# Two accumulator tiles for the attention, a turned gate column, and weight splits with a fixed place: three edits to one block kernel

## The chip, the cores and the metric

The kernel runs on one core of one Trainium2 chip. The core's engines are TensorE (PE in the profile; PEld is its weight load), VectorE (DVE), ScalarE (ACT), GpSimd (POOL) and SyncE (SP). DMAs are issued from the queues of SP, ACT and POOL. The metric is the device time of one execution in microseconds; a kernel's time is the median of several runs. Beside these runs stands one profiled execution, from which every trace number comes.

## The reference

The reference is one block of a diffusion backbone: 512 latent tokens and 256 context tokens, model width 2048, one layer, float32.

```python
shift, scale, gate = jnp.split(silu_c @ w_ada[l] + b_ada[l], 3, axis=-1)
h = _modulate(_rmsnorm(xs, norm_g[l]), shift[:, None], scale[:, None])
...
p = h @ w_l
q = _rope(_rmsnorm(_heads(p, OFF_Q, N_Q_HEADS), q_norm_g[l]), cos, sin) * q_scale
k = _rope(_rmsnorm(_heads(p, OFF_K, N_KV_HEADS), k_norm_g[l]), cos, sin)
...
attn = _attention(q, jnp.concatenate([k, kc], axis=1), jnp.concatenate([v, vc], axis=1))
...
y_a = (attn * jax.nn.silu(z_a)) @ w_pa
y_b = (_fourier_mix(u_b) * jax.nn.silu(z_b)) @ w_pb
y = (g_a * y_a + g_b * y_b) @ w_o
new_xs = xs + gate[:, None] * y
```

A modulated norm feeds one wide projection. Of it come queries (12 heads of 128), keys and values (4 heads), two SiLU gates, two sigmoid gates and the input of a Fourier mixing. The attention runs over 768 keys. Each branch is projected to 2048, the two are merged by their sigmoid gates, and after one more projection the result is multiplied by "gate", a vector of 2048 numbers, added to the input and normed.

## The kernel before

**Products.** Every large product is exact to float32 by three float32r matmuls (mm3, lines 339 to 341): each factor is split into a high and a low part, and high x high, high x low and low x high are added up in one accumulator. The split itself (split_from, lines 181 and 182) is a ScalarE copy that writes the high part and a VectorE subtraction that writes the low one. It is done on chip for weights (tiles "whi" and "wlo" from a raw piece "wr" or "R" of 128x1024) and for activations.

**Weight stream.** All weights come through one list, "todo", of pieces in the order of use. load_more issues the loads while raw buffers are free; get(key) returns a split piece and on the way splits some pieces ahead of it (split_piece, line 265 on). A split needs one of three pairs of hi/lo buffers.

**Stages.** The trace shows the norm and the first products up to about 160 us, the eight groups of the large projection up to 803 us, the attention up to about 1005 us, and then branch A, the merge and the output projection up to the end. The projection groups keep their sums in the pool "psp" (names x and y, four pairs of two banks, which are the whole of PSUM). When they end, that pool is closed and "psq" is opened on the same eight banks: one tile "banks" of 128 x 8 x 512, of which banks[0] is the first six and banks[1] the last two. `wide` are four areas of 768 columns in the first six: three take scores in turn (next_wide), the fourth takes the turned probabilities. Bank 6 (fill_acc) is the accumulator of the Fourier branch; bank 7 takes the values' products and the turned queries.

**The attention's loop** runs over 48 steps, 12 heads by 4 blocks of 128 queries. A step holds: the scores of block i with their maximum (VectorE, L1533) and exponential (ScalarE, L1535); the values of an earlier pair of blocks; the turning of block i-1 (turn: six TensorE transposes, L1551, into the fourth wide area, then a split into "pth" by ScalarE and "ptl" by VectorE); the division of block i-1; and one or two of the 64 steps of the Fourier branch's projection (filler, fill). That projection runs over four chunks of 512 columns, in the order 0, 2, 1, 3; a chunk takes two weight pieces (key "pab") and 16 steps of three matmuls. At steps 10, 22 and 34 the keys and values of the next key head are fetched (get_keys), and with them the next chunk's two pieces are split ahead. At 16 of the steps a product of weights with the conditioning row (use_gate, L1369) leaves one column of the vector "gate" in gparts.

**After the loop** the two halves of gparts and a bias are added into gcol (128 x 16: number 128k+p of the vector stands in partition p, column k), and gcol is stored to the DRAM tile gs (16 x 128) on POOL's queue, in the order of gs's columns (L1744 to L1746). load_rows reads gs later as rows, spread over all partitions (L1783).

**What sets the order.** A planner places each engine's instructions from its own model of their durations, before anything runs; the order in the program is its priority. Within a manual_schedule block the order is that of the program; issue_after(i) queues what the block traces behind instruction i on i's engine, without waiting for i's end. PE is in manual order before the projection groups; in the attention nothing is, apart from a few issue_after. Each engine works its instructions strictly in the order planned, and waits at each for its semaphores. A pool with reuse_waits="tile" makes a tile wait for the former tiles that lay where it lies, and not for a whole former pool.

Of the kernel before, what the change touches and what calls it, by code (L numbers as in the profile page):

```python
# [10 lines left out]
F32 = mybir.dt.float32  # L11
F32R = mybir.dt.float32r
ACT = mybir.ActivationFunctionType
ALU = mybir.AluOpType
# [4 lines left out]
P = 128  # L19
# [3 lines left out]
KK = D // P  # L23
# [4 lines left out]
NKEY = T + C  # L28
KT = NKEY // P
# [44 lines left out]
def context_piece(g, name, pc):  # L74

    n = 28 * (g - NQZ) + 4 * ONE_GROUP.index(name) + pc
    if n % 2 == 0 and 0 <= n < 8:
        return "cn", n // 2
    if n % 7 == 4 and 18 <= n < 46:
        return "cr", n // 7 - 2  # L80
# [43 lines left out]
def block_kernel(ctx, tc, xT, ctx_rows, ctx_toks, x, c_row, w_ss, w_gate, vecs, qkg, rope, dft_c, dft_s,  # L124
                 w_start, w_g, w_pab, w_o, final_g, out):
    nc = tc.nc
# [6 lines left out]
    const = sb("const")  # L133
# [9 lines left out]
    gs = dsc.tile([KK, P], F32, name="gs")  # L143
# [13 lines left out]
    def uid(s):  # L157
        cnt[0] += 1
        return f"{s}{cnt[0]}"
# [20 lines left out]
    def split_from(src, hi, lo):  # L180
        first = nc.scalar.activation(hi, src, ACT.Copy)  # L181
        return first, nc.vector.tensor_tensor(lo, src, hi.bitcast(F32), op=ALU.subtract)  # L182
# [61 lines left out]
    def hl_tiles():  # L244
        if more_hl and not more_hl[0]:
            hl_pools.extend(range(MORE_HL))
            more_hl.clear()
        elif more_hl:
            more_hl[0] -= 1
        hl_pools.append(hl_pools.pop(0))  # L250
        pool = hl_pools[-1]
        if isinstance(pool, tuple):
            return [slot_tile(p, (1024,), F32R) for p in pool]
        if isinstance(pool, int):
            return int_tiles(pool)
        return [pool.tile([P, 1024], F32R, tag=t, bufs=hl_pools.count(pool), name=uid("w" + t)) for t in ("hi", "lo")]


    last_split, split_of, in_line, context_sub, chained = [], [], [], [], []

    look = [1]

    def split_piece(e):
        if e.out is not None or e.kind == "raw":
            return
        raws = [r for _, r in e.raws]
        src = raws.pop(0) if e.stage is None else chain[e.pc]
        for r in raws:
            nc.vector.tensor_tensor(src, src, r, op=ALU.add)
        if e.off:  # L270
            with ExitStack() as line:
                if e.key == ("P7", KV, 3):
                    line.enter_context(tc.issue_after(context_sub[-1].ins))
                if e.key[1] in DIFF_IN_LINE:

                    line.enter_context(tc.issue_after(split_of[-2][1].ins))
                nc.vector.tensor_tensor(src, chain[e.pc], src, op=ALU.subtract)
        hi, lo = e.dst() if e.dst else hl_tiles()
        if isinstance(hi, Halves):
            for k in range(2):  # L280
                last_split.append(split_from(src[:, 512 * k : 512 * k + 512].rearrange("p (a c) -> p a c", a=2),
                                             hi.parts[k], lo.parts[k]))
        else:
            hi, lo = hi[:, : e.cols], lo[:, : e.cols]
            with ExitStack() as line:
                if in_line:
                    for i in last_split[-1]:
                        line.enter_context(tc.issue_after(i.ins))
                last_split.append(split_from(src, hi, lo))
        split_of.append(last_split[-1])  # L290
        if e.nxt is not None:
            chained[:] = [nc.gpsimd.dma_start(chain[e.pc], e.nxt, accum_op=ALU.add)]  # L292
        if e.stage == 3:
            left[e.pc] = 0
        r = lambda t: t if isinstance(t, Halves) else t.rearrange("p (n m) -> p n m", n=e.n)
        e.out = (r(hi), r(lo))

    def get(key):
        load_more()
        turn = [e for e in ahead if not e.aside]  # L300
        assert turn[0].key == key, (turn[0].key, key)
        for e in turn[: min(look[0], len(hl_pools))]:
            if e is turn[0] or e.key[0] != "V":
                split_piece(e)
        load_more()
        e = turn[0]
        ahead.remove(e)
        free.extend(p[0::2] for p, _ in e.raws if p in retired)
        return e.raws[0][1] if e.kind == "raw" else e.out
# [17 lines left out]
    def take(shape, dt=F32, pool=None):  # L327
        p = next((p for p in free if p[0] is pool), free[0])
        free.remove(p)
        t = slot_tile(p, shape, dt)  # L330
        home[id(t)] = p, t
        return t

    def give(*ts):
        free.extend(home.pop(id(t))[0] for t in ts)
# [19 lines left out]
    cvt, bada, ng = small[:, : 2 * KK], small[:, 2 * KK : 5 * KK], small[:, 5 * KK :]  # L355
# [1 line left out]
    nc.vector.tensor_scalar(bsc1, bada[:, KK : 2 * KK], 1.0, None, op0=ALU.add)  # L357
    shift = const.tile([P, KK, 2], F32, name="shift")
    gain = const.tile([P, KK, 2], F32, name="gain")
    gcol = const.tile([P, KK], F32, name="gcol")  # L360
    gparts = const.tile([P, 2 * KK], F32, name="gparts")

    pairs = []
# [58 lines left out]
    for g in range(LAST + 1):  # L422
        for name in ONE_GROUP:
            if (g, name) == (LAST, "Q4"):
                stream_keys(0)
            if g == KV:
                f = CTX_FORMS.index(next(f for n, f, _, _ in PRODUCTS if n == name))
                stream(("cf", name), cf_d[:, :, f].rearrange("i p j c -> p i j c"), 1024, 8, dst=ctx_tiles)
            stream_product(name, g, w_g[g], BY_DVE_GATES if g else ())
            for pc in range(4):  # L430
                p = context_piece(g, name, pc)
# [4 lines left out]
            for pc in range(4):  # L436
                if (g, name, pc) in GATE_AT:
                    q = GATE_AT[g, name, pc]
                    stream(("gate", q), w_gate[q], 1024, 1, "raw")
                    e = todo.pop()  # L440
# [4 lines left out]
    q = NGATE  # L445
# [300 lines left out]
    def split_next():  # L746
        e = next(e for e in ahead if e.out is None and e.kind != "raw")
        split_piece(e)
        e.raws = []
# [27 lines left out]
    with tc.manual_schedule(engines={E.PE}):  # L777
# [6 lines left out]
        with tc.manual_schedule(engines={E.Activation, E.DVE}):  # L784
# [25 lines left out]
            for kb in range(1, 4):  # L810
                k = kb + 1
# [32 lines left out]
            for kb in range(4, KK - 4, 2):  # L844
# [6 lines left out]
                k = kb + 2  # L851
# [100 lines left out]
    for g in range(4):  # L952
        gate_b(g)
        positions(g)
        if g < 2:
            tokens(g + 2)
        with behind((finals[-1], low[g if g < 2 else 3])):
            for e in ahead[:g]:
                split_piece(e)
            for z, y in products[2 * g - 4 : 2 * g - 2] if g > 1 else ():  # L960
                nc.vector.tensor_tensor(z, y, z, op=ALU.mult)
# [18 lines left out]
    banks = []  # L980
# [478 lines left out]

    pgs.close()  # L1460
    psq = ctx.enter_context(tc.tile_pool(name="psq", bufs=1, space=PSUM, reuse_waits="tile"))
    whole_psum = psq.tile([P, 8, 512], F32, name="banks")
    banks += [whole_psum[:, :6, :], whole_psum[:, 6:, :]]
    last_y[:] = [0, 0]
    wide = [flat(banks[0])[:, NKEY * i : NKEY * i + NKEY] for i in range(4)]
    fill_acc, b1 = banks[1][:, 0, :], lambda: banks[1][:, 1, :]
# [49 lines left out]
    probs, pts, AT, A1, A2 = {}, {}, {}, {}, {}  # L1516
# [30 lines left out]
    def turn(i):  # L1547
        p = probs.pop(i)
        tp = wide[3]
        for k in range(KT):  # L1550
            nc.tensor.transpose(tp[:, k * P : (k + 1) * P], p[:, k * P : (k + 1) * P], ident)  # L1551
        if i % 2 == 0:
            pts[i // 2] = [atp.tile([P, KT, 256], F32R, tag=n, bufs=2, name=uid(n)) for n in ("pth", "ptl")]
        c = slice((i % 2) * P, (i % 2) * P + P)
        split_from(tp[:, :NKEY].rearrange("p (k q) -> p k q", k=KT), *(w[:, :, c] for w in pts[i // 2]))
        give(p)

    def values(half):
# [127 lines left out]
    for i in range(NSTEP + 3):  # L1686
# [13 lines left out]
        if 1 <= i <= NSTEP:  # L1700
            turn(i - 1)
            divide(i - 1)
# [5 lines left out]
        n = next((n for n, at in enumerate(SUM_AT) if at <= i < at + 3), None)  # L1708
# [8 lines left out]
        if i == 3:  # L1717
            with tc.issue_after(maxima[0].ins), tc.issue_after(maxima[1].ins):
                e = take((1024,))
# [8 lines left out]
        if i in GATE_STEPS:  # L1728
            n = NGATE + GATE_STEPS.index(i)
# [11 lines left out]
            next(first)  # L1741
    ats_.close()
    left[3] = 0
    nc.vector.tensor_tensor(gcol, gparts[:, :KK], gparts[:, KK:], op=ALU.add)  # L1744
    nc.vector.tensor_tensor(gcol, gcol, bada[:, 2 * KK :], op=ALU.add)
    nc.gpsimd.dma_start(gs.rearrange("k p -> p k"), gcol)  # L1746


    gp = ctx.enter_context(tc.tile_pool(name="gp", bufs=1, side="right", reuse_waits="tile"))
# [320 lines left out]
```

## Time and profile before

| | |
|---|---|
| median of 3 runs | 1285.94 us (1285.69 to 1288.67) |
| profiled execution | 1286.97 us, span of its instructions 1285.2 us, granted clock 0.999 |
| TensorE | 1269.6 us busy, 6562 matmuls |
| VectorE, ScalarE, GpSimd | 991.0, 683.2 and 173.2 us busy |
| DMA | 319.07 MB, mean 248 GB/s |

How to read the lines: "L339 PE MATMUL banks<-whi,s" is line 339 of the kernel, an instruction of TensorE that writes the tile "banks" and reads "whi" and "s" (numbers in tile names are left out). In a timeline the columns are the start and the duration in us, the engine and the instruction; behind it, in brackets, the idle time of the engine just before and what ended it ("<-ACT ev L1160"). A matmul's record is longer than its share of the stream, since the next one begins before it ends.

### The profile page before, as it was taken

What the parts mean: (1) busy time and instruction counts of PE and PEld (TensorE: products, weight loads), DVE (VectorE), ACT (ScalarE), POOL (GpSimd) and SP (SyncE); (2) the same over time, 40 slices, a digit from 0 to 9 for tenths busy, and PEclk for the clock granted to TensorE, in tenths of its full rate; (3) what the DMA queues carried; (4) which work ended last, traced back from release to release, by engine and by line L of the source; (5) the groups of instructions that cost most, each with busy time, mean ns of one, the idle gap of its engine ahead of it and who ended that gap; (6) DMA issues with size and microseconds to landing.
All of it is one profiled execution on the core that took longest, in us unless ns stands there. A gap on an engine that the chain in (4) does not pass through costs nothing.

```text
span 1285.2 us, 17638 instructions
## 1 busy us (share of the span) xinstructions
PE 1269.6 (99%) x6562; PEld 1045.2 (81%) x6562; DVE 991.0 (77%) x1305; ACT 683.2 (53%) x1077; POOL 173.2 (13%) x226
## 2 busy tenths in 40 slices
PE   8999999999999999999999999999999999999997
PEld 5677888888888888888888888888888888888886
DVE  5767899889778787748687756778898777787677
ACT  5322765555466564543355445766667646465544
POOL 0000121111102011012021011011100221211310
PEclk9999999999999999999999999999999999999999
DMA  9998798888898998887879897578852989998986
GB/s 378 412 368 344 242 204 254 229 240 239 234 315 209 320 271 254 291 197 188 282 204 288 254 259 234 180 234 250 265 178 67 260 241 258 245 207 222 227 207 179
DMA packets 104343, 319.07 MB, mean 248 GB/s; under 512 B 9889, under 2 KB 32801, under 8 KB 100289
## 3 DMA queue, kind: packets, MB, share of 16 engines
q1 hardware_dynamic: 54336, 195.24, 41.8%
q0 software_dynamic: 27600, 100.29, 37.0%
q10 hardware_dynamic: 22320, 22.42, 5.1%
q8 instruction: 51, 0.84, 0.3%
q14 instruction: 36, 0.29, 0.1%
HBM read 283.30 MB, written 34.61 MB: 247 GB/s over the span
## 4 chain that ended last, share of the span: by engine, by line
PE 82%; DVE 3%; DMA 2%; ACT 2%; issue 1%; SPq 0%; ACTq 0%
PE banks L339 10%; PE banks L340 10%; PE banks L341 10%; PE x L341 9%; PE x L339 9%; PE x L340 9%; PE y L341 8%; PE y L340 8%; PE y L339 8%; PE banks L1551 2%; DMA wr<-in_w_pab 1%; DVE wlo L182 1%; DMA s<-yb_d 1%; PE banks L1665 1%; DVE s L182 0%
## 5 line engine op out<-in xcount | busy, mean ns | idle before, releaser
L181 ACT ACTIVATE whi<-R 128x1024 fp32r<-128x1024 f32 x138 | 145.1, 1058 | 143.7 <-PE banks L341 47.5
L182 DVE TENSOR_TENSOR wlo<-R,whi 128x1024 fp32r<-128x1024 f32 x138 | 167.7, 1221 | 61.2 <-ACT whi L181 60.9
L182 DVE TENSOR_TENSOR wlo<-wr,whi 128x1024 fp32r<-128x1024 f32 (+1 forms) x122 | 147.3, 1213 | 62.7 <-ACT whi L181 62.5
L181 ACT ACTIVATE whi<-wr 128x1024 fp32r<-128x1024 f32 (+1 forms) x122 | 127.4, 1050 | 123.4 <-PE y L341 33.0
L339 PE MATMUL banks<-whi,s 128*128 128x512 f32 (+1 forms) x400 | 157.8, 394 | 0.9 <-ACT ev L1160 0.7
L340 PE MATMUL banks<-wlo,s 128*128 128x512 f32 (+1 forms) x400 | 155.9, 390 | 0.0
L341 PE MATMUL banks<-whi,s 128*128 128x512 f32 (+1 forms) x400 | 155.8, 389 | 0.0
L339 PE MATMUL x<-whi,s 128*128 128x512 f32 x352 | 137.1, 390 | 0.0
L341 PE MATMUL x<-whi,s 128*128 128x512 f32 x352 | 137.0, 389 | 0.0
L340 PE MATMUL x<-wlo,s 128*128 128x512 f32 x352 | 136.9, 389 | 0.0
L292 POOL DMA_DIRECT2D R<-in_w_g x68 | 59.5, 874 | 484.7 <-DVE wlo L182 290.2
L340 PE MATMUL y<-wlo,s 128*128 128x512 f32 x316 | 123.0, 389 | 0.1
L339 PE MATMUL y<-whi,s 128*128 128x512 f32 x316 | 122.9, 389 | 0.0
L341 PE MATMUL y<-whi,s 128*128 128x512 f32 x316 | 122.8, 389 | 0.0
L181 ACT ACTIVATE s<-wr 128x512 fp32r<-128x512 f32 (+2 forms) x93 | 60.8, 677 | 66.0 <-DMA wr<-cf_d 24.4
L182 DVE TENSOR_TENSOR s<-wr,s 128x512 fp32r<-128x512 f32 (+2 forms) x93 | 66.7, 749 | 31.8 <-ACT s L181 30.9
L339 PEld LDWEIGHTS banks<-whi,s 128*128 128x128 f32 x400 | 75.2, 188 | 16.6 <-ACT ev L1160 1.1
L341 PEld LDWEIGHTS banks<-whi,s 128*128 128x128 f32 x400 | 75.2, 188 | 15.3
L340 PEld LDWEIGHTS banks<-wlo,s 128*128 128x128 f32 x400 | 75.2, 188 | 13.9 <-DVE wlo L182 0.2
L340 PEld LDWEIGHTS x<-wlo,s 128*128 128x128 f32 x352 | 66.1, 188 | 13.8
L341 PEld LDWEIGHTS x<-whi,s 128*128 128x128 f32 x352 | 66.1, 188 | 13.7
L339 PEld LDWEIGHTS x<-whi,s 128*128 128x128 f32 x352 | 66.1, 188 | 13.6
(333 smaller groups left out, 2794.0 us busy)
## 6 DMA issues: line engine op xcount, KB each, us to landing
wr<-in_w_g SPq DMA_DIRECT2D x124, 512.0 KB, 5.6
R<-in_w_g POOLq DMA_DIRECT2D x68, 512.0 KB, 7.4
wa<-in_w_ss SPq DMA_DIRECT2D x31, 1024.0 KB, 9.5
R<-in_w_g SPq DMA_DIRECT2D x32, 512.0 KB, 5.8
wr<-in_w_gate SPq DMA_DIRECT2D x32, 512.0 KB, 5.1
wr<-in_w_o SPq DMA_DIRECT2D x24, 512.0 KB, 7.1
R<-in_w_o POOLq DMA_DIRECT2D x24, 512.0 KB, 8.9
wr<-in_w_pab SPq DMA_DIRECT2D x20, 512.0 KB, 6.1
```

The source lines that it names most:

```text
L181: first = nc.scalar.activation(hi, src, ACT.Copy)
L182: return first, nc.vector.tensor_tensor(lo, src, hi.bitcast(F32), op=ALU.subtract)
L292: chained[:] = [nc.gpsimd.dma_start(chain[e.pc], e.nxt, accum_op=ALU.add)]
L339: nc.tensor.matmul(o, ah, bh, start=start, stop=False, skip_group_check=cont)
L340: nc.tensor.matmul(o, ah, bl, start=False, stop=False, skip_group_check=cont)
L341: nc.tensor.matmul(o, al, bh, start=False, stop=stop, skip_group_check=cont)
L1551: nc.tensor.transpose(tp[:, k * P : (k + 1) * P], p[:, k * P : (k + 1) * P], ident)
L1665: last_turn[0] = nc.tensor.transpose(tp[:, k // 2, 256 * (k % 2) + P * t : 256 * (k % 2) + P * t + P], m[:, t, k * P : k * P + P], ident)
```

## The change

Three edits stand together.

1. The tile "banks" of eight banks becomes two tiles, of six and of two banks, at the same place. All views into them stay.
2. gcol becomes 128 x 32. The additions go in place into gparts, VectorE transposes gparts into gcol (blocks of 32 x 32: within each block of 32 partitions, column k becomes row k), and four DMAs on POOL's queue store rows of 32 numbers, 16 rows each, in place of the one.
3. Each turn's pair of split instructions is kept in the list turned_low. When a piece with the key "pab" is split, its two instructions are queued behind the pair that is the third last in the list at that time, ScalarE's behind ScalarE's and VectorE's behind VectorE's. For the first chunk's pieces the list is empty and nothing is queued.

```diff
-    last_split, split_of, in_line, context_sub, chained = [], [], [], [], []
+    last_split, split_of, in_line, context_sub, chained, turned_low = [], [], [], [], [], []
...
             with ExitStack() as line:
-                if in_line:
-                    for i in last_split[-1]:
-                        line.enter_context(tc.issue_after(i.ins))
+                for i in last_split[-1] if in_line else turned_low[-6:-4] if e.key[0] == "pab" else ():
+                    line.enter_context(tc.issue_after(i.ins))
                 last_split.append(split_from(src, hi, lo))
...
-    gcol = const.tile([P, KK], F32, name="gcol")
+    gcol = const.tile([P, 2 * KK], F32, name="gcol")
...
-    whole_psum = psq.tile([P, 8, 512], F32, name="banks")
-    banks += [whole_psum[:, :6, :], whole_psum[:, 6:, :]]
+    banks += [psq.tile([P, n, 512], F32, name=f"banks{n}") for n in (6, 2)]
...
-        split_from(tp[:, :NKEY].rearrange("p (k q) -> p k q", k=KT), *(w[:, :, c] for w in pts[i // 2]))
+        turned_low.extend(split_from(tp[:, :NKEY].rearrange("p (k q) -> p k q", k=KT), *(w[:, :, c] for w in pts[i // 2])))
...
-    nc.vector.tensor_tensor(gcol, gparts[:, :KK], gparts[:, KK:], op=ALU.add)
-    nc.vector.tensor_tensor(gcol, gcol, bada[:, 2 * KK :], op=ALU.add)
-    nc.gpsimd.dma_start(gs.rearrange("k p -> p k"), gcol)
+    nc.vector.tensor_tensor(gparts[:, :KK], gparts[:, :KK], gparts[:, KK:], op=ALU.add)
+    nc.vector.tensor_tensor(gparts[:, :KK], gparts[:, :KK], bada[:, 2 * KK :], op=ALU.add)
+    nc.vector.transpose(gcol, gparts)
+    for i in range(0, P, 32):
+        nc.gpsimd.dma_start(gs[:, i : i + 32], gcol[i : i + KK, :])
```

## The prediction, written before the result was known

> **What bounds the kernel now.** I read the page first: the busy line, the clock, the chain.
>
> ```profile
> PE 1269.6 (99%) x6562; PEld 1045.2 (81%) x6562; DVE 991.0 (77%) x1305; ACT 683.2 (53%) x1077; POOL 173.2 (13%) x226
> ...
> PEclk9999999999999999999999999999999999999999
> ...
> PE 82%; DVE 3%; DMA 2%; ACT 2%; issue 1%; SPq 0%; ACTq 0%
> ```
>
> TensorE works from end to end at full clock, and the chain lies on it for 82%. None of the three edits takes a matmul away, so all that can be won is time in which TensorE waits. The next view is the busy time by stretches (columns: length; then PE, PEld, DVE, ACT, POOL busy with counts; clock; DMA share; GB/s).
>
> ```profile
> 320.00:480.00 160.00, 160.00 (x710) 132.53 (x709) 128.01 (x179) 89.33 (x146) 20.45 (x22) 1.00 0.91 268
> 800.00:1010.00 210.00, 207.42 (x1363) 181.18 (x1363) 174.84 (x280) 143.01 (x272) 28.65 (x47) 1.00 0.65 195
> 1000.00:1100.00 100.00, 100.00 (x488) 84.17 (x487) 75.60 (x73) 56.06 (x61) 22.13 (x29) 1.00 0.97 257
> ```
>
> The projections (320 to 480 us) and the stage behind the attention (1000 to 1100 us) have no idle TensorE time; the attention (800 to 1010 us) has 210 - 207.42 = 2.58 us. The first row gives a yardstick too: 710 matmuls in 160 us are one each 0.225 us, while one record lasts 0.39 us (rows below). So a record covers the first 0.39 - 0.225 = 0.16 us of any gap, and a wait costs its idle time and 0.16 us. The third view lists TensorE's own waits from 800 us on, then from 1010 us on:
>
> ```profile
> PE banks L1389 <- DVE ptl L182: 0.8, 1, 0.8
> PE banks L339 <- ACT ev L1160: 0.7, 1, 0.7
> PE banks L1551 <- DVE ptl L182: 0.4, 1, 0.4
> PE banks L339 <- ACT s L1535: 0.4, 1, 0.4
> PE banks L339 <- DVE R L1499: 0.2, 1, 0.2
> ...
> PE banks L1665 <- DMA s<-yb_d: 0.7, 1, 0.7
> ```
>
> Five waits in the attention sum to 2.5 us, with 5 x 0.16 some 3.3 us; the one behind it is 0.9 us. That is all there is to see for a change of this kind: 4.2 us, 0.33% of the time.
>
> **Part 1, the banks as two tiles.** The timeline where the last projection group gives way to the attention:
>
> ```profile
> 795.39 0.69 DVE L182 TENSOR_TENSOR s<-y,s 128x512 fp32r<-128x512 f32 x1 [2.03 <-ACT s L181]
> ...
> 802.54 0.39 PE L341 MATMUL x<-whi,s 128*128 128x512 f32 x1
> ...
> 802.97 0.59 ACT L1160 COPY ev<-x 128x512 f32<-128x512 f32 x1 [1.66 <-PE x L341]
> ...
> 803.60 0.50 PE L339 MATMUL banks<-whi,s 128*128 128x512 f32 x1 [0.68 <-ACT ev L1160]
> ...
> 805.10 0.28 PE L339 MATMUL banks<-s,s 128*128 128x256 f32 x1
> ```
>
> The first matmul into "banks" comes 1.06 us after the last into "x", where 0.225 would do: 0.83 us lost. It is a matmul of the Fourier branch, and goes to bank 6 alone; but the one tile of eight banks stands on all the old accumulators and waits for the last reader of any, here ScalarE's copy out of an x. As two tiles, the two-bank one waits only for whoever held banks 6 and 7. The old pool made its two x pairs first, then the y pairs, so I take it for a y, whose last reader ended at 795.39 + 0.69 = 796.1. Then the six Fourier matmuls (803.60 to 805.10) start at 802.77 and cover the copy, which ends at 803.56; the scores, in the six-bank tile, find it done. If that cover were gone (the scores planned ahead of them), the wait would merely move to the scores. Bounds: -0.83 (cover holds) and 0 (an x lies there after all, or the order turns). I take -0.83: nothing in the row makes the six need more than bank and weights. No instruction is added.
>
> **Part 2, the gate columns.** It removes one DMA of 128 x 16 single numbers, adds one VectorE transpose of a 128x32 tile and three more DMAs on POOL's queue. The rows of today, in order: the second of the two additions, the store, the next POOL load; then the store's time to landing; then the first reader.
>
> ```profile
> 988.37 0.18 DVE L1745 TENSOR_TENSOR gcol<-gcol,small 128x16 f32<-128x16 f32 x1
> ...
> 989.01 1.20 POOL L1746 DMA_DIRECT2D gs<-gcol  x1 [14.92 <-DVE gcol L1745]
> 991.95 0.90 POOL L292 DMA_DIRECT2D R<-in_w_pab  x1 [1.74 <-DVE wlo L182]
> ...
> gs<-gcol POOLq DMA_DIRECT2D x1, 8.0 KB, 11.2
> ...
> 1091.87 0.55 POOL L1783 DMA_DIRECT2D s<-gs  x1 [5.30 <-DVE s L182]
> ```
>
> The store lands at 1000 us and is first read at 1091.87: 91 us cover whatever its time becomes, and 8 KB in 11.2 us can shrink only behind that cover. VectorE's transpose is not in the trace; the nearest rows bound it: 0.18 us (128x16) below, 0.42 us (the 128x256 subtractions) above. I take 0.2 us by its size; it falls where TensorE shows no wait, so 0 on the path, 0.42 if it meets one. POOL's four issues at 0.55 to 0.90 us are 2.2 to 3.6 us against 1.20: from 989.2 they end by 992.8, and the weight load at 991.95 goes out at most 0.9 us late. Its product is in the stage that has no idle time and a DMA share of 0.97 from 1000 us on, so -0.9 to +0.9 is the bound. I take 0.
>
> **Part 3, the splits behind their steps.** A Fourier weight piece is split in two by ScalarE (whi) and VectorE (wlo). Eight are split in all, in the order in which the branch uses them; these rows are of the whole, then of the fifth:
>
> ```profile
> L181 ACT ACTIVATE whi<-wr x8: 1049/1061/1077, 797.5 to 940.3; 128x1024 fp32r<-128x1024 f32 x8
> ...
> 836.09 6.13 DMA wr<-in_w_pab
> ...
> 842.30 1.07 ACT L181 ACTIVATE whi<-wr 128x1024 fp32r<-128x1024 f32 x1 [1.66 <-DMA wr<-in_w_pab]
> 843.27 0.88 ACT L1535 ACTIVATE s<-banks,gain 128x768 f32<-128x768 f32 x1
> ...
> 844.14 0.80 ACT L181 ACTIVATE pth<-banks 128x768 fp32r<-128x768 f32 x1
> ...
> 842.30 0.87 PE L1551 MATMUL banks<-ident,s 128*128 128x128 f32 x6 [0.40 <-DVE ptl L182]
> ...
> 845.99 0.44 PE L1389 MATMUL banks<-ident,wr 128*128 128x128 f32 x2 [0.82 <-DVE ptl L182]
> ```
>
> ScalarE stands 1.66 us for a load still under way; queued behind it are the next exponential and the next turned split (pth, 844.14), then VectorE's ptl, then TensorE at 845.99: 0.82 + 0.16 = 0.98 us. TensorE's other wait here, 0.40 + 0.16, ends at 842.30, before ScalarE goes on, so that load is not its cause. And nobody needs that piece yet: it is the first of the third chunk, the 33rd of the branch's 64 steps, and by 887.3 only 30 were done.
>
> ```profile
> L339 PE MATMUL banks<-whi,s x16: 389/395/501, 803.6 to 840.2; 128*128 128x512 f32 x16
> 847.27 0.40 PE L339 MATMUL banks<-whi,s 128*128 128x512 f32 x1
> ...
> L339 PE MATMUL banks<-whi,s x30: 387/396/501, 803.6 to 887.3; 128*128 128x512 f32 x30
> ...
> L181 ACT ACTIVATE pth<-banks x7: 807/812/815, 811.4 to 836.3; 128x768 fp32r<-128x768 f32 x7
> ...
> L181 ACT ACTIVATE pth<-banks x19: 802/812/815, 811.4 to 883.6; 128x768 fp32r<-128x768 f32 x19
> ...
> L181 ACT ACTIVATE pth<-banks x31: 802/812/816, 811.4 to 932.2; 128x768 fp32r<-128x768 f32 x31
> ```
>
> The pieces are split in the program at steps 10, 22 and 34, where 9, 21 and 33 score blocks have been turned; the pair [-6:-4] of the list is the third last of these: turns 6, 18, 30 (counted from 0), at 836.3, 883.6, 932.2. So the second chunk's two pieces may go from 837 (ScalarE) and 839 (VectorE), and at 1.2 us each on VectorE are done by 841.4; their first use is the 17th step, at 847.27: 5.9 us cover. The third chunk goes behind 883.6, the fourth behind 932.2. No queue is passed and no DMA added; raw buffers are held longer (the second chunk's first until 840), so what waits on SP for a free one starts later; late next would be a gate product or the next group's keys, and the planner's order on SP decides which. No row prices that; I let part 2's 0.9 us stand for it in the range. The sum by place:
> - 830 to 848: two splits now (pieces 4, 5), two after (3, 4), both landed long ago. The DMA wait goes: -0.98, and -1.54 if piece 4, now at 834, had made the other one. Two splits back to back put 1.2 us more between a pth and its ptl: +0.2 (1.2 - 0.98) at worst. I take -0.8, near the row of the removed wait.
> - 880 to 900: likewise two and two, without this wait:
>
> ```profile
> 895.38 1.06 ACT L181 ACTIVATE whi<-wr 128x1024 fp32r<-128x1024 f32 x1 [1.23 <-DMA wr<-in_w_pab]
> 897.87 0.50 PE L339 MATMUL banks<-whi,s 128*128 128x512 f32 x1 [0.22 <-DVE R L1499]
> 930.00:950.00 20.00, 19.64 (x132) 17.04 (x131) 18.32 (x30) 14.31 (x28) 2.01 (x4) 1.00 0.55 178
> ```
>
> TensorE's 0.22 + 0.16 goes: -0.4; bounds -0.4 and 0.
> - 930 to 950: one split now (the last), two after. VectorE is busy 18.32 of 20 us, and another 1.2 us leaves 0.5. Bounds 0 and +1.4 (1.2 + 0.16). A step's share of VectorE has 0.7 us free (174.84 busy of 210, over 48 steps of 4.4); I take +0.5, what is left of 1.2.
>
> Both waits, at 842.30 and 845.99, end with ptl, which frees the one area that score blocks are turned in. The Trainium skill ("Perfetto Trace Analysis", Optimization Strategy) reads the same gap recurring on the engine that should be saturated as a sign that there is not enough SBUF or PSUM for the next tile; by it the gap would come back at another step, and the sum would be 0.8 us less of a gain. The trace agrees for the 0.40 us at 842.30, which no load wait precedes, and not for the 0.82 us at 845.99, which one does.
>
> **Sum:** -0.83 + 0 - 0.8 - 0.4 + 0.5 = -1.5 us. The profiled execution took 1286.97 (span 1285.2 and 1.8 around it), 1.0 above the median of the runs, 1285.94. It would become 1285.5, and the median **1284.4**. A measurement of this kernel can tell about 0.3% from no change, 3.9 us here, so this is "no change". One cost stays out of the sum: the planner orders the attention anew from its own durations, which may move any small wait.
>
> **Rivals.**
> 1. **All waits go** (0.25). With no split in the way the planner's order holds: all five attention waits, 3.3, the branch wait, 0.9, and part of the gaps under 0.16 us that records cover (48 steps, at most 7.7; a sixth is 1.3): -5.5, 1280.4. For it: each wait is on a DVE or ACT that runs late. Against: the 0.4 us on L1535 and the one on yb_d have nothing to do with the edits.
> 2. **The wait comes back** (0.15). The one turning area is what limits: TensorE's wait for ptl returns a step later whatever ScalarE did, so only -0.83 and +0.5 are left: 1285.6. For it: both waits end with ptl. Against: the longer one has the load wait ahead of it. This is how the time would go by the Trainium skill's rule quoted above. That the whole change does nothing falls here too.
> 3. **Slower: the splits bunch** (0.10). With 0.7 us of VectorE free in a step, a split of 1.2 us needs two steps, and two need four. Where the planner puts both within fewer, next to the keys' split and a gate product (1.2 us), each split between pth and ptl holds TensorE 1.2 us. Four of the six so placed cost +4.9, less 0.83: 1290.0. It decides from two splits in under four steps, at 837, 885 or 933 us. For it: VectorE at 18.32 of 20. Against: today a gate product and a split stand back to back at 834, and TensorE's next wait comes 6 us later (842.30).
>
> ```profile
> 833.64 1.22 DVE L1369 SCALAR_TENSOR_TENSOR wr<-wr,crow 128x1024 f32<-128x1024 f32 x1
> ...
> 834.86 1.21 DVE L182 TENSOR_TENSOR wlo<-wr,whi 128x1024 fp32r<-128x1024 f32 x1
> ```
>
> **How the numbers follow.** The forecast has 0.50, its own range 1282.3 (-0.83 - 1.54 - 0.4 - 0.9 = -3.7) to 1288.8 (0 + 0.2 + 0 + 1.4 + 0.9 + 0.4 = +2.9), each with all bounds at one end. Low end of the range: rival 1 and part 2's 0.9, 1279.5. High end: just above the forecast's own, 1289.0, which leaves out rival 3 at its full price. Faster by over 0.3%: rival 1 and a tail of the forecast below 1282.1, 0.28. Slower: rival 3, 0.09. Within: the rest, 0.63.
>
> **What would show it.** Part 1: a first "banks" matmul 0.2 us behind the last x one, no wait on L1160. Part 2: gs landing in under 6 us and nothing else moved. Part 3: whi from wr in pairs behind turns 6, 18 and 30, none waiting for in_w_pab; TensorE idle in the attention under 1.5 us instead of 2.58. It is wrong if new waits on ptl stand at 837 to 848 or 932 to 948, or if the stage behind 1010 us moves by more than 1 us.

## The result, and the profile after: 15% slower

The changed kernel takes 1477.46 us (median of 5 runs, 1473.18 to 1477.97); the kernel before, run beside it, 1286.18 us. The ratio is 1.1476, 95% interval 1.1459 to 1.1494: 191 us slower, where 1284.4 us was forecast. The page of the changed kernel (busy line; then TensorE's busy tenths and its clock in 40 slices of 36.9 us):

```profile
span 1474.0 us, 17650 instructions
...
PE 1335.2 (91%) x6562; PEld 1079.9 (73%) x6562; DVE 1000.2 (68%) x1306; ACT 690.6 (47%) x1077; POOL 173.8 (12%) x229
...
PE   8999999999999999999999767777777988898996
...
PEclk9999999999999999999999888989988999999998
```

The 6562 matmuls are the same. The first 22 slices (to 811 us) are as before; then TensorE is idle about a quarter of the time in the attention, and its clock falls. Of the span's growth, 1474.0 - 1285.2 = 188.8 us, TensorE's idle time is (1474.0 - 1335.2) - (1285.2 - 1269.6) = 123.2 us, and its longer busy time 1335.2 - 1269.6 = 65.6 us. Two stages hold nearly all of it. The attention's 48 turned splits mark them, here of the kernel before, then of the changed one (minimum, median and maximum in ns; first and last start):

```profile
L181 ACT ACTIVATE pth<-banks x48: 796/812/828, 811.4 to 1003.7; 128x768 fp32r<-128x768 f32 x48
```

```profile
L181 ACT ACTIVATE pth<-banks x48: 792/810/815, 813.6 to 1143.7; 128x768 fp32r<-128x768 f32 x48
```

From the first to the last: 192.3 us before, 330.1 after, or 4.09 and 7.02 us a step (47 intervals): +137.8. From the last to the end of the span: 281.5 and 330.3: +48.8. With the 2.2 us up to the first that is 188.8. TensorE's largest waits in the changed kernel, four in the attention and one behind it (us in total, times, longest):

```profile
PE banks L338 <- DVE ptl L182: 49.0, 44, 2.9
PE banks L1549 <- ACT s L1533: 20.0, 15, 2.1
PE banks L338 <- ACT pth L181: 10.3, 12, 1.2
PE banks L1388 <- DVE ptl L182: 5.4, 3, 1.8
...
PE banks L338 <- DVE s L1108: 15.2, 6, 4.8
```

In the attention before, these were five waits of 2.5 us in all. Lines are one or two lower than before (338 for 339, 1549 for 1551, 1533 for 1535). One round of the attention shows what they are, in the timeline:

```profile
815.46 0.51 PE L338 MATMUL banks<-s,s 128*128 128x512 f32 x1 [0.81 <-DVE ptl L182]
...
816.81 0.96 DVE L1531 TENSOR_REDUCE gain<-banks 128x1 f32<-128x768 f32 x1 [1.41 <-PE banks L340]
...
817.80 0.90 ACT L1533 ACTIVATE s<-banks,gain 128x768 f32<-128x768 f32 x1 [3.40 <-DVE gain L1531]
...
818.85 1.54 PE L1549 MATMUL banks<-ident,s 128*128 128x128 f32 x6 [2.08 <-ACT s L1533]
...
820.43 0.81 ACT L181 ACTIVATE pth<-banks 128x768 fp32r<-128x768 f32 x1 [1.00 <-PE banks L1549]
821.27 0.96 DVE L182 TENSOR_TENSOR ptl<-banks,pth 128x768 fp32r<-128x768 f32 x1 [2.28 <-ACT pth L181]
...
822.28 0.58 PE L338 MATMUL banks<-s,s 128*128 128x256 f32 x1 [0.41 <-DVE ptl L182]
```

Read it as a ring: scores, maximum (816.81), exponential (817.80), turn (818.85), pth, ptl, next scores (822.28). That is 1.35 + 0.99 + 1.05 + 1.58 + 0.84 + 1.01 = 6.82 us, and each link begins when the one ahead of it ends. Two links carry no data. The turn at 818.85 turns the *previous* block, whose exponential was done a step ago; it waits for the exponential of the *newest* block. And the scores at 822.28 go to an area of their own, yet wait for ptl, which reads the turning area. What the two ends share is the six-bank tile.

### The profile page after: what moved, and what is told of

It is laid out like the page before. It is cut to its first block, busy times and chain, and to the rows that moved or that the text cites. A ratio compares the mean times of both kernels' runs of the same rounds, so it can differ in the third digit from the quotient of the medians.

```text
span 1474.0 us, 17650 instructions
## 1 busy us (share of the span) xinstructions
PE 1335.2 (91%) x6562; PEld 1079.9 (73%) x6562; DVE 1000.2 (68%) x1306; ACT 690.6 (47%) x1077; POOL 173.8 (12%) x229
## 5 line engine op out<-in xcount | busy, mean ns | idle before, releaser
L338 PE MATMUL banks<-whi,s 128*128 128x512 f32 (+1 forms) x400 | 166.1, 415 | 33.8 <-DVE s L1108 15.2
L339 PE MATMUL banks<-wlo,s 128*128 128x512 f32 (+1 forms) x400 | 161.5, 404 | 0.0
L340 PE MATMUL banks<-whi,s 128*128 128x512 f32 (+1 forms) x400 | 161.1, 403 | 0.0
L339 PE MATMUL y<-wlo,s 128*128 128x512 f32 x316 | 123.2, 390 | 0.0
L338 PEld LDWEIGHTS banks<-whi,s 128*128 128x128 f32 x400 | 79.2, 198 | 58.2 <-ACT whi L181 15.1
L338 PE MATMUL banks<-s,s 128*128 128x512 f32 (+1 forms) x160 | 66.9, 418 | 46.1 <-DVE ptl L182 46.1
L1533 ACT ACTIVATE s<-banks,gain 128x768 f32<-128x768 f32 x48 | 43.2, 901 | 130.0 <-DVE gain L1531 129.8
L340 PEld LDWEIGHTS banks<-whi,s 128*128 128x128 f32 x400 | 78.6, 197 | 17.3
L339 PEld LDWEIGHTS banks<-wlo,s 128*128 128x128 f32 x400 | 79.3, 198 | 14.6
L182 DVE TENSOR_TENSOR ptl<-banks,pth 128x768 fp32r<-128x768 f32 x48 | 45.9, 957 | 64.6 <-ACT pth L181 64.4
```

Of the source, the lines that this page charges most:

```text
L338: nc.tensor.matmul(o, ah, bh, start=start, stop=False, skip_group_check=cont)
L339: nc.tensor.matmul(o, ah, bl, start=False, stop=False, skip_group_check=cont)
L340: nc.tensor.matmul(o, al, bh, start=False, stop=stop, skip_group_check=cont)
L1533: maxima[1] = nc.scalar.activation(probs[i], sc[:, :NKEY], ACT.Exp, bias=mx[:, 0:1], accum_out=mx[:, 1:2])
```

## The experiments

**Theory A**: a write of TensorE into a tile that holds only some of the eight banks waits for every earlier reader of *any* bank of that tile, while accesses to the one tile of eight were told apart by bank (or by finer pieces, which no run here separates). In the six-bank tile this ties turns and scores into the ring. **Rival B**: the ties of the splits, or the order that the planner makes of them, carry the loss. **C**: the parts hurt only together. Where an expectation below says A1 and A2, A1 holds that the two waits cost so much only as a closed ring, A2 that each has a price of its own.

All runs; ratios are to the kernel before beside them, and the last two columns are from the profiled executions, as above: first to last pth, last pth to the end.

| kernel | median, us | ratio (95%) | attention | behind |
|---|---|---|---|---|
| before | 1285.69 to 1286.25 | | 192.3 | 281.5 |
| changed | 1477.46 | 1.1476 (1.1459-1.1494) | 330.1 | 330.3 |
| e1 tiles only | 1480.64 | 1.1515 (1.149-1.154) | 331.6 | 330.4 |
| e2 gate and ties | 1285.73 | 0.9997 (0.9989-1.0006) | 190.1 | 281.9 |
| e3 gate only | 1285.97 | 0.9999 (0.999-1.0008) | 191.1 | 280.9 |
| e4 ties only | 1290.85 | 1.0038 (1.0024-1.0052) | 190.0 | 286.8 |
| e5 scores wait | 1313.63 | 1.0215 (1.0186-1.0245) | 217.6 | 283.1 |
| e6 turns wait | 1290.98 | 1.0037 (1.0021-1.0053) | 194.0 | 283.3 |
| e7 both wait | 1380.78 | 1.0738 (1.0685-1.0791) | 280.9 | 283.0 |
| e10 all wait | 1425.87 | 1.109 (1.1051-1.1129) | 332.2 | 283.9 |
| e8 one tile, cut | 1292.22 | 1.005 (1.003-1.007) | 189.2 | 290.4 |
| e9 four tiles | 1297.93 | 1.0093 (1.0064-1.0123) | 196.3 | 290.2 |
| e12 turn apart | 1348.32 | 1.0487 (1.0466-1.0508) | 221.0 | 314.4 |
| e11 store late | 1286.01 | 1.0001 (0.9991-1.0011) | 190.7 | 281.5 |
| e13 store held | 1295.00 | 1.0064 (1.0046-1.0082) | 191.2 | 290.2 |
| e14 cut, rows | 1285.18 | 0.9993 (0.9983-1.0002) | 189.2 | 283.9 |
| e15 four, rows | 1298.14 | 1.0091 (1.0075-1.0107) | 196.2 | 290.5 |

### Which part: e1 to e4

e1 is the kernel before with this alone:

```diff
-    whole_psum = psq.tile([P, 8, 512], F32, name="banks")
-    banks += [whole_psum[:, :6, :], whole_psum[:, 6:, :]]
+    banks += [psq.tile([P, n, 512], F32, name=f"banks{n}") for n in (6, 2)]
```

> The kernel before with the banks as two tiles of six and two banks, and nothing else of the change. Theory A (a write into a tile that holds only some of the eight banks waits for every earlier reader of any bank of that tile, so each score block waits for the split of the turned block before it, and each turn for the exponential of the newest score block): this part alone carries the loss, 1465 to 1485 us, and TensorE's waits between 803 and 1160 us again stand on ptl and on s, some 90 us. Theory B (the ties of the weight splits, or the new order of the attention that they bring, carry it): 1284 to 1288 us. Theory C (the parts only hurt together): 1300 to 1420 us.

1480.64 us, and the same waits:

```profile
PE banks L339 <- DVE ptl L182: 47.9, 44, 2.9
PE banks L1550 <- ACT s L1534: 22.3, 17, 2.6
```

Part 1 is the whole loss. e2 is the rest of the change, without part 1:

> The gate columns and the tied splits, with the banks left as one tile of eight. Theory A: no loss, 1281 to 1288 us, by the prediction's terms for these two parts -0.7 us against the kernel before; the wait on L1160 (0.7 us) is back at 803 us. Theory B: 1440 to 1480 us. Theory C: under 1290 us.

1285.73 us, no change. TensorE's waits from 800 us on are two:

```profile
PE banks L1664 <- DMA s<-yb_d: 0.7, 1, 0.7
PE banks L338 <- ACT ev L1159: 0.7, 1, 0.7
```

B and C fall: neither this run nor e1 shows a loss that needs the ties. e3 is part 2 alone, e4 part 3 alone:

> The gate columns alone. By the prediction's second part 0 us, bounds -0.9 to +0.9: a ratio of 0.9993 to 1.0007 to the kernel before. The store of the gates lands in under 6 us instead of 11.2.

> The tied splits alone. By the prediction's third part -0.7 us (-0.8 at the first pair, -0.4 at the second, +0.5 at the last), bounds -1.9 to +1.6: a ratio of 0.9985 to 1.0012. The whi splits from wr stand in pairs behind turns 6, 18 and 30, and none waits for its load. Its rival (the wait on the one turning area comes back a step later): the same time as before, with TensorE's idle time in the attention still 2 us or more.

e3 came as expected: no change; each of its four row stores landed 1.5 to 1.6 us after its issue. e4 did not: +4.9 us (3.1 to 6.7), outside the bounds. The attention is no slower (190.0 us); the 5 us are lost behind it, where TensorE now waits for a load from yb_d:

```profile
1035.48 1.24 PE L1664 MATMUL banks<-ident,s 128*128 128x128 f32 x8 [2.69 <-DMA s<-yb_d]
```

The last group of experiments is about that.

### Are the two false waits the loss: e5, e6, e7, e10

These keep the one tile of eight banks and the old layout, and add the waits as true dependencies, which the planner sees.

The first edit is e5's (mm3 returns its first matmul, ptl_of lists the ptl splits), the second e6's; e7 has both, and e10 has both without the conditions "a == 0" and "k == 0", so on both halves of a score block and on all six transposes.

```diff
+    def wait_for(ins, other):
+        tc.add_manual_dep(ins.ins, other.ins.name, ...)
...
-            mm3(sc[:, a:b], qh, ql, kh[:, a:b], kl[:, a:b], True, True)
+            first = mm3(sc[:, a:b], qh, ql, kh[:, a:b], kl[:, a:b], True, True)
+            if a == 0 and ptl_of:
+                wait_for(first, ptl_of[-1])
```

```diff
-            nc.tensor.transpose(tp[:, k * P : (k + 1) * P], p[:, k * P : (k + 1) * P], ident)
+            turned = nc.tensor.transpose(tp[:, k * P : (k + 1) * P], p[:, k * P : (k + 1) * P], ident)
+            if k == 0:
+                wait_for(turned, maxima[1])
```

> One tile of eight banks as before; added is one wait per score block: its first matmul waits for the newest split ptl of a turned block. Theory A1 (the two new waits cost so much only together, as they close a loop from scores over exponential, turn and ptl to the next scores): under 1320 us alone. Theory A2 (each wait has its own price, as TensorE's waits of the changed kernel sum up, 49 + 4 us on ptl before scores): 1330 to 1350 us.

> One tile of eight banks as before; added is one wait per step: the turn waits for the newest exponential, that of the score block behind its own. A1: under 1320 us alone. A2: 1300 to 1320 us (20 us of waits on s before turns in the changed kernel).

> One tile of eight banks as before, with both waits added. A1: 1400 to 1450 us, some 7 us for each of the 48 steps as in the changed kernel (the split of eight into six and two banks is then not needed for the loss in the attention; what the changed kernel loses behind 1155 us, some 40 us, stays away). A2: 1350 to 1375 us. If the loss comes from something else about two tiles (where they lie, the order of the work): under 1300 us.

Alone they cost 27 and 5 us (25.3 and 1.7 of it in the attention); together 94.5. So A1 holds in kind: two waits that close the ring cost far more than the sum of both. That a single one leaves the planner room to put other work ahead of it is my reading, not shown by a run of its own. And 1380.78 is short of A1's 1400 and over A2's 1375. The timeline of e7 shows why: the wait sat on one transpose, and the planner pulled others of the same turn ahead of it.

```profile
935.90 0.60 PE L1560 MATMUL banks<-ident,s 128*128 128x128 f32 x4
...
938.19 0.20 PEld L1560 LDWEIGHTS banks<-ident,s 128*128 128x128 f32 x2 [0.24 <-ACT s L1544]
938.19 0.44 PE L1560 MATMUL banks<-ident,s 128*128 128x128 f32 x2
```

So e10 puts the wait on every one:

> The trial with both waits, but with the wait on every transpose of a turn and on both halves of a score block (in the earlier trial the planner pulled up to four of the six transposes and half of the scores ahead of the one waiting instruction). If the two waits, kept whole, are the loss in the attention: 1425 to 1445 us (1286 and the 147 us that the changed kernel loses before 1155 us), and the stage behind the last pth at 281 to 284 us as before. If the rest comes from something else that shares a tile: 1375 to 1395 us.

```profile
L181 ACT ACTIVATE pth<-banks x48: 795/810/814, 812.2 to 1144.4; 128x768 fp32r<-128x768 f32 x48
```

1425.87 us, and an attention of 332.2 us where the changed kernel has 330.1: with one tile, the old layout and old order of the program, the two waits alone are enough for the attention's whole loss. (That the two figures lie within 2 us is partly luck: e10's two runs are 8.5 us apart, and the profiled one is the slower.) The stage behind stays at 283.9 us, so the changed kernel's 48.8 us there are a loss of their own.

### What shares a tile: e9, e12

Both cut the banks into pairs with a use each: two score areas (in place of three), the turning area, and the last pair as before. e9 makes a tile of each pair (the diff); e12 puts both score areas into one tile of four banks, beside two tiles of two.

```diff
-    whole_psum = psq.tile([P, 8, 512], F32, name="banks")
-    banks += [whole_psum[:, :6, :], whole_psum[:, 6:, :]]
+    banks += [psq.tile([P, 2, 512], F32, name=f"banks{n}") for n in range(4)]
...
-    wide = [flat(banks[0])[:, NKEY * i : NKEY * i + NKEY] for i in range(4)]
+    wide = [flat(banks[i])[:, :NKEY] for i in range(3)]
```

> The kernel before with the banks as four tiles of two banks each: two score areas (not three), the turning area, and the Fourier and context banks, each in a tile of its own, so that a wait for any reader of the tile is nearly always one for the data's own reader. Theory A (what shares a tile decides, not how many tiles there are): 1284 to 1320 us, where the upper end is the price of two score areas and of Fourier steps that wait for the context's reader in the shared last tile. Rival (tiles smaller than eight banks cost by themselves): 1450 us or more.

> Three tiles: two score areas together in one of four banks, the turning area alone in one of two, the last pair in one of two. If the loop through turn and ptl is the loss, taking the turning area out of the scores' tile breaks it, and what is left is that a score block waits for the exponential of the one before: 1295 to 1340 us. If any sharing of a tile by score areas costs as much: 1380 us or more.

e9 loses 11.7 us and not 190: tiles smaller than eight banks are not slow by themselves. e12, outside its expected range by 8 us, loses 28.7 us in the attention (221.0 - 192.3: the ring without the turn, in which a score block waits for the exponential of an earlier one, the first line below) and 32.9 behind it. There the accumulators of the next products are pairs of the same banks. In e12 two of them share a tile, in e9 none do. Below stand TensorE's largest wait in e12's attention and its two largest behind, then e9's largest behind:

```profile
PE banks L339 <- ACT s L1535: 8.9, 12, 1.7
...
PE banks L339 <- DVE s L1109: 11.0, 3, 4.8
PE banks L1665 <- DMA s<-yb_d: 5.2, 3, 3.7
```

```profile
PE banks L339 <- ACT s L1114: 2.4, 2, 1.7
```

e12's 5.2 us for a load from yb_d are another matter: it issued the store of single numbers, the subject of the last group, at 1016.85, and whether that made the load late no run tests. The changed kernel, where three accumulators share one tile, has the wait on the finished sums six times (L1108 there, 15.2 us). Its trace shows one:

```profile
1191.26 1.23 DVE L1108 TENSOR_TENSOR s<-banks,s 128x1024 f32<-128x1024 f32 x1 [0.40 <-PE banks L340]
1192.40 1.22 DVE L182 TENSOR_TENSOR wlo<-wr,whi 128x1024 fp32r<-128x1024 f32 x1
1193.53 1.22 DVE L1108 TENSOR_TENSOR s<-s,s 128x1024 f32<-128x1024 f32 x1
1194.66 1.22 DVE L1108 TENSOR_TENSOR s<-s,banks 128x1024 f32<-128x1024 f32 x1
...
1196.03 0.76 PE L338 MATMUL banks<-whi,s 128*128 128x512 f32 x1 [4.81 <-DVE s L1108]
```

The next product waits until VectorE has read the finished sums of the others, 4.81 us. The data don't ask for it: the kernel before, with the same pairs in the same order of the program, has no wait of TensorE on these sums.

So A stands for the attention: what shares a tile decides. For the 48.8 us behind it the cause is shown in part. e1 loses them too (330.4 against 281.5 us), so the two tiles make them, and the 15.2 us are of the kind above; of the rest, shorter waits and a lower clock are in the trace, and no run takes them apart. Why accesses to a tile of all eight banks are told apart, and to a smaller one are not, is in no trace.

### The store of single numbers: e4, e8, e11, e13, e14, e15

e8 was to be the partner of e9, the same layout as one tile:

> One tile of eight banks, but with the layout of the kernel with four tiles (two score areas of two banks, the turning area, the last pair). If the 11.7 us of the four tiles are the price of a score area less, 1295 to 1300 us here too; if they are what tiles of two banks cost by themselves, 1285 to 1288 us.

1292.22 us, between the two, and again behind the attention (290.4 us), with one wait for yb_d of 5.17 us. In e4 and e8 the planner had issued the gate columns' store at 1003.53 and 1004.40 us, where the kernel before has it at 989.01; e2 has the four row stores at 1005.19 and waits 0.7 us for yb_d, as the kernel before does. So I suspected the store. e11 was to move it alone, by queueing the additions ahead of it behind the last exponential (issue_after).

> The kernel before, with only the two additions and the store of the gate columns held behind the last exponential, so that the store goes out at 1002 to 1004 us as in the kernel with the ties alone, and not at 989. If the 5 us that the ties alone lost come from the store of single numbers in that place: 1289 to 1292 us, a landing of s<-yb_d of over 15 us and a wait for it on TensorE. If they come from the ties: 1285 to 1287 us.

The store went at 988.68: the edit moved nothing, since the exponential is ScalarE's, the additions VectorE's, and issue_after orders one engine's queue. The run says nothing on the question. One run speaks against a price in every case: e6 issued the old store at 1002.33, ahead of its last pth, and TensorE waited 0.4 us for yb_d. e13 makes the first addition wait for that exponential in truth:

```diff
-    nc.vector.tensor_tensor(gcol, gparts[:, :KK], gparts[:, KK:], op=ALU.add)
+    late = nc.vector.tensor_tensor(gcol, gparts[:, :KK], gparts[:, KK:], op=ALU.add)
+    tc.add_manual_dep(late.ins, maxima[1].ins.name, ...)
```

> The kernel before, with the first of the two additions of the gate columns waiting for the last exponential of the attention, so that the store of single numbers goes out at some 1002 to 1005 us and not at 989. If that store, in that place, is what cost the ties alone 5 us: 1288 to 1292 us, a landing of s<-yb_d of over 15 us, and TensorE waiting for it. If it was the ties: 1285 to 1287 us, and no such wait.

1295.00 us, 8.9 more than before and even over the range. What the DMAs moved in slices of 1.5 us from 980 to 1040 us, then the times to landing in that stretch, in e13 and then in e2:

```profile
GB/s 0 0 96 371 235 8 0 0 66 139 254 399 221 153 208 309 229 131 52 295 29 46 25 38 25 30 22 260 415 410 328 270 298 421 358 268 276 219 205 218
```

```profile
R<-in_w_pab SPq DMA_DIRECT2D x1, 512.0 KB, 16.5
s<-yb_d POOLq DMA_DIRECT2D x1, 512.0 KB, 21.3
gs<-gcol POOLq DMA_DIRECT2D x1, 8.0 KB, 14.5
```

```profile
GB/s 0 202 388 117 3 0 0 71 183 279 371 175 177 254 254 279 66 177 202 300 391 407 325 172 213 232 221 202 213 273 273 268 369 426 330 221 213 202 213 279
```

```profile
R<-in_w_pab SPq DMA_DIRECT2D x1, 512.0 KB, 6.6
s<-yb_d POOLq DMA_DIRECT2D x1, 512.0 KB, 8.5
gs<-gcol POOLq DMA_DIRECT2D x4, 2.0 KB, 3.0
```

For seven slices, 10.5 us, 22 to 46 GB/s are all that moves, where e2 moves 172 to 407. With a store of 8 KB on the way, loads of 512 KB land late, SP's as well as POOL's, and TensorE stands 6.62 us for the one from yb_d:

```profile
1039.73 1.97 PE L1665 MATMUL banks<-ident,s 128*128 128x128 f32 x8 [6.62 <-DMA s<-yb_d]
```

e14 and e15 are e8 and e9 with the row store:

> One tile of eight banks in the cut layout (two score areas) with the gate columns stored as rows. If the store of single numbers at 1004 us made the 6.4 us of this layout: 1285 to 1288 us, and no wait of 5 us for yb_d. If the layout itself did: 1291 to 1293 us.

> The same layout and the row store, with four tiles of two banks. In the trial of four tiles the store went at 989 us, so the row store should change little: 1295 to 1299 us. What lies between this and the one tile of the same layout is the price of tracking by whole tile where nearly every tile has one use: by TensorE's waits of the earlier trial (4.8 us on ptl, 2.4 + 1.2 on s behind the attention) some 8 to 12 us; if it is under 3 us, that price is not there and the place of the store made the difference.

e14 gains back 7.0 us and is level with before: neither the cut layout nor a score area less costs anything that can be measured. e15 stays at 1298.14. Same layout, same store, same chip: 1298.14 - 1285.18 = 13.0 us is what tracking by whole tile costs in four tiles, 7.0 us in the attention and 6.6 behind it; somewhat over the 8 to 12 I expected.

No kernel here beats the one before by more than its interval; e14 and e2 come nearest.

## Why the prediction was wrong

**Part 1 failed, and all else with it.** The step that failed is its term for the two tiles, bounded by "-0.83 (cover holds) and 0", with "No instruction is added". Alone, in e1, that term measured +195 us (1480.64 - 1285.69). It looked at one wait only, the one in which the new tile takes over its banks from the old pool, and there it was right in each detail. In the changed kernel's timeline:

```profile
802.75 0.39 PE L340 MATMUL x<-whi,s 128*128 128x512 f32 x1
802.98 0.39 PE L338 MATMUL banks<-whi,s 128*128 128x512 f32 x1
```

The first "banks" matmul comes 0.23 us behind the last x one, as foretold, and the wait for ev is gone. What was not asked is what the *other* accesses of a tile wait for once its outline changes. The same split that let one write pass by a reader in another tile put every pair of accesses within a tile under one roof: 188.8 us in place of -0.83. No instruction is added indeed; waits are. No rival held this either: the cases moved waits that load and weight splits cause, and none had a wait that the tile itself makes. Slower by over 0.3% had a chance of 0.09, all of it for rival 3's bunched splits, and the range's high end, 1289.0, rested on the small bounds of parts 2 and 3 and left even rival 3's price out.

**Part 2** was sized rightly: 0 forecast, 0.9999 (0.999 to 1.0008) measured in e3; the transpose took 0.21 us (0.2 taken), the four issues 1.9 us (2.2 to 3.6), the rows landed in 1.5 to 4.0 us, "under 6". But its reason, that "91 us cover whatever its time becomes", was too weak: it asked who reads gs, and not which loads the store holds up. At 989 that went well by luck: in the kernel before, too, only 19 to 63 GB/s moved from 995 to 1002.5 us, and the store of 512 KB to yb_d issued at 996.28 took 12.2 us to land (4.1 in e2), but TensorE waited for nothing of it longer than 0.7 us. At 1003.5 to 1007.7 (e4, e8, e13) the old store costs 5 to 9 us, and the row store is what keeps part 3 free of that.

**Part 3** did what was foretold, seen in e2: ScalarE's whi from wr in pairs at 835.95 (two), 882.44 and 886.75, 931.41 and 938.18, none waiting for its load, and TensorE 210 - 209.25 us idle in the attention ("under 1.5"):

```profile
800.00:1010.00 210.00, 209.25 (x1372) 183.84 (x1371) 177.16 (x286) 144.04 (x275) 29.53 (x50) 1.00 0.65 203
```

The waits that split loads had caused went, and did not come back a step later, so e2's trace speaks against rival 2. Its time can't: the size forecast for parts 2 and 3 (-0.7) lies within e2's interval, -1.4 to +0.8 us, and so does no change. The sentence "one cost stays out of the sum: the planner orders the attention anew" is where e4's 5 us came from: the ties moved the store by 14 us, and with the old store that is dear.

**"It is wrong if ... the stage behind 1010 us moves by more than 1 us"** named a true sign; it grew by 48.8. New waits on ptl, the other sign, came all through the attention. The rule of the Trainium skill ("Perfetto Trace Analysis", Optimization Strategy) that a gap recurring on the engine which should be busy can mean too little PSUM for the next tile would point the reader of the changed trace to more buffers. The trace does not agree: the areas are the same four as before, and e10 has waits on ptl and on s of the same kind with the old tile.

## What to carry to other kernels

A tile can also be the unit in which its accesses are ordered; here it was for tiles of two, four and six banks, and not for the tile of eight. Before a tile is split or merged, list for each of its writers who else reads the new tile, and see whether a ring comes out: here two waits that cost 27 and 5 us alone made 94.5 together, and 140 where no instruction could slip past them, because they closed a loop over three engines. Areas that are in use at the same time belong in tiles of their own or, 13 us better here (e14 against e15), in a tile whose accesses are told apart; of a moved or reshaped store, ask not only who reads it, but which loads are in flight beside it.

## What the runs showed that I had not expected

**The clock fell with waits of 2 us.** In the changed kernel none of the waits in the attention that are shown above is longer than 2.9 us, yet the granted clock, the third column from the end in the busy times by stretches, is lower there:

```profile
1000.00:1100.00 100.00, 73.23 (x391) 59.91 (x392) 55.23 (x87) 42.68 (x78) 4.76 (x9) 0.88 0.31 100
```

Matmuls of 512 columns on both sides of a change of the clock, in the timeline:

```profile
929.88 0.40 PE L339 MATMUL banks<-s,s 128*128 128x512 f32 x1
930.11 0.39 PE L340 MATMUL banks<-s,s 128*128 128x512 f32 x1
...
930.70 0.63 PE L338 MATMUL banks<-whi,s 128*128 128x512 f32 x1
931.12 0.63 PE L339 MATMUL banks<-wlo,s 128*128 128x512 f32 x1
```

The distance from start to start goes from 0.23 to 0.42 us. The turn quoted above, at 818.85, already runs so: 1.54 us for six transposes, against 0.88 where the clock is up:

```profile
939.77 0.88 PE L1549 MATMUL banks<-ident,s 128*128 128x128 f32 x6
```

The Trainium skill ("TensorE: Matmul & The Clock Gate", What's actually happening) has two rates, half and full, and the fall to half after an idle window of some 3.4 us. The half rate agrees with 0.42 against 0.23. The idle window does not: in the 3.4 us ahead of 818.85 TensorE worked from 815.46 to 816.8, where the maximum of its scores begins. In this trace the granted clock is at half for 109.9 us in all, and TensorE is busy in 89.6 of them; at full clock that work would take about half as long, so some 45 us (an estimate) are lost to the clock, the larger part of the 65.6 us of longer busy time. Here recurring gaps cost more than their length.

**Eight kilobytes can hold up half-megabyte loads.** While 2048 single numbers, 8 KB, were being stored in e13, the core's transfers fell to 22 to 46 GB/s for 10.5 us, where e2 has 172 to 407 in the same slices; in e2 the same numbers, as 64 rows of 32, landed in 3.0 us (median of the four stores).
